# Hybrid DeltaNet and differential-attention block: where in a partition the moving operands of the 256-column products begin

## The chip, the cores and the metric

The kernel runs on one core of one Trainium2 chip. The metric is the device time of one execution, in microseconds. The kernel before takes 1933.78 us, the median of three runs (1933.39 to 1934.75 us).

A matrix product on TensorE has two operands in on-chip memory. One, here called the loaded operand, is put into the array ahead of the product (128 columns of it, an instruction of its own, shown as engine PEld). The other, the moving operand, streams through it (up to 512 columns). While one product streams, the operand of the next is being loaded.

## The reference, cut to what matters

One layer of a hybrid backbone over 1024 latent tokens with 256 context tokens ahead of them, model width 1024. One wide projection feeds two branches: a chunked gated DeltaNet with a short convolution (A) and a differential softmax attention with eight heads (B). Both are gated, projected, merged and mapped out.

```python
h = rms_norm(x) * (1.0 + scale[:, None]) + shift[:, None]
hc = rms_norm(ctx) * (1.0 + scale_c) + shift_c
qkv_a, z_a, a_raw, b_raw, q_b, k_b, v_b, z_b, gates = split_cols(h @ w_in)
...
o_a, o_ac = gdn_bidirectional(...)            # branch A
...
def block(qi):                                # branch B, 128 queries at a time
    s = jnp.einsum('bqhcd,bkhcd->bhcqk', qi, k).astype(jnp.float32) * scale
    p = jax.nn.softmax(s, axis=-1)
    attn = p[:, :, 0] - lam * p[:, :, 1]
    return jnp.einsum('bhqk,bkhv->bqhv', attn.astype(v.dtype), v)
...
merged = g_a * (y_a.reshape(b, length, GDN_WIDTH) @ w_oa) + g_b * (y_b.reshape(b, length, DIFF_V_WIDTH) @ w_ob)
return merged @ w_out
```

## The kernel before, in words

**Products in three passes.** The large products are made of float32r parts: each operand is split into a high part and a low remainder, and three products are summed, high by high, high by low and low by high. So for every block of 128 rows of the contraction there are three products.

**Two ways round.** For most of the projection the weights are loaded and the normed tokens `hs` move, 512 columns at a time (for the convolved q, k and v of branch A, and for the gates). For q, k and v of branch B it is the other way round: 128 tokens of `hs` are loaded and the weights `wh`, `wl` (high and low parts of 256 columns of the projection, tiles of 8 x 256 floats in a partition) move. These are the 256-column products of `part_flow`, and of the second column group of kind "t" in `conv_flow`. The first group of that kind carries 32 more columns for the gates of branch A, so its products have 288 columns.

**The stages, in the order of the profile.** The front (norms, modulation, the first weights), then the conv stage with 512-column products and the two groups of kind "t"; the parts stage to 734 us (four pairs of k, two of v, four of q, with the preparation of branch A between them), which the second group of kind "t" precedes from 398 us on; the scan stage to about 1290 us (the chunk recurrence `chain`, `out` in 128-column products, with the gate projections of 512 columns filling in); attention to about 1764 us (scores `s`, transposes `t`, values `v`, and the products `ma` of the projection of branch A filling in); then `mb` and the last projection `x`, `z`.

**Attention.** For each head and 128 queries, six pieces of scores: the queries' high part `qh` and then their low part `ql` is loaded, the keys `kk` move (512, 512 and 256 columns, for each of two softmaxes). VectorE scales the scores and takes their minimum (L1571), ScalarE exponentiates, VectorE, ScalarE and GpSimd combine the two softmaxes, TensorE transposes the result, ScalarE and VectorE split it in `ah` and `al` (L1640, L1645). For two blocks of 128 queries together, `att_out` makes 30 products of 256 columns: `vh` or `vl` loaded, `ah` or `al` moving.

**What sets the order.** The kernel orders its instructions itself while it is built. Every stream of work is a generator that names the engine, a cost and what it waits for, and a planner with modelled clocks takes the next one; the costs are numbers in the code (0.1195 for a product of 256 columns) and do not come from tile addresses. Semaphores are set by the framework from the tiles' places.

**Where tiles lie.** A pool gives each tag a place in every partition. The weights' tiles come from two pools, `wa` and `wb`; the queries, keys, values and softmax tiles from `a0`, `a1`, and for even heads the high queries and keys from the pool of branch A's preparation. In the program as built, the moving operand of each 256-column product of `part_flow`, of the second group of kind "t" and of `att_out` begins a whole multiple of 128 bytes away from the operand that is loaded while it streams. That also holds for the 512-column products of the projections. In the scores of even heads, the low queries `ql` begin 64 bytes off a multiple of 128 from the keys that stream while they are loaded; in those of odd heads they do not.

## Time and profile before

| what | value |
|---|---|
| median of three runs | 1933.78 us |
| the profiled execution's own time | 1933.29 us |
| its span, first to last instruction | 1931.2 us |
| granted TensorE clock | 1.000 |
| products on TensorE (records) | 13807 |
| 256-column products with weights moving (`mm<-wh,hs`, `mm<-wl,hs`) | 1632 + 816 |
| 256-column products with softmax tiles moving (`v<-ah`, `v<-al`) | 640 + 320 |
| the same weights moving with 288 columns | 160 + 80 |

How to read it: the records of products overlap, since the next product begins to stream before the last results of the one before have come out. A record's duration is therefore not what a product costs in a full stream; that is the distance from one start to the next. In the names, `out<-moving,loaded` for products and the same names for the loads (engine PEld). Waits of TensorE are those that end on another engine; two matters look alike in busy time, a wait inside the array and the streaming itself.

### The profile page before, as it was taken

The page shows a single profiled execution, that of the slowest core. Times are in us where ns is not written, and L with a number is a line of the kernel's source. Part 1 is how long each engine was busy: PE and PEld are TensorE (multiplying, and loading weights), DVE is VectorE, ACT ScalarE, POOL GpSimd, SP SyncE. Part 2 cuts the span into 40 slices and gives each one's busy share as a digit, 9 for nine tenths or more (in the row PEclk, how much of TensorE's full clock was granted, in tenths as well). Part 3 has the DMA queues.
Part 4 walks back from the last instruction along what each step waited for, and adds up shares of the span by engine and source line. Part 5 has one row for each costly group of instructions (what it writes and reads, how often), then busy time and mean ns, then how long its engine had stood idle before and what let it go on. Part 6 is the DMA issues. An engine that isn't in the chain of part 4 may idle for free.

```text
span 1931.2 us, 37500 instructions
## 1 busy us (share of the span) xinstructions
PE 1890.5 (98%) x13807; PEld 1665.9 (86%) x13807; DVE 1450.8 (75%) x3613; ACT 1075.3 (56%) x2237; POOL 678.1 (35%) x610
## 2 busy tenths in 40 slices
PE   6999999999999999999999999999999999999999
PEld 4888888899999998888888888888997888888887
DVE  4687998957887888867865865338996979995677
ACT  4543444426233564677576656448885868884222
POOL 3200000005441342343333332326766667672203
PEclk9999999999999999999999999999999999999999
DMA  9144535575545557667785575666336474226542
GB/s 335 60 135 98 138 95 136 124 193 175 166 142 182 183 191 229 227 195 234 210 290 176 196 200 154 219 226 225 131 123 208 158 240 150 92 88 213 191 153 87
DMA packets 383038, 336.39 MB, mean 174 GB/s; under 512 B 142609, under 2 KB 323443, under 8 KB 381831
## 3 DMA queue, kind: packets, MB, share of 16 engines
q1 hardware_dynamic: 382855, 333.99, 55.1%
q8 instruction: 109, 1.79, 0.4%
q14 instruction: 74, 0.61, 0.1%
HBM read 222.14 MB, written 111.79 MB: 173 GB/s over the span
## 4 chain that ended last, share of the span: by engine, by line
PE 82%; DVE 7%; DMA 4%; ACT 4%; issue 2%; POOL 1%; SPq 1%; ACTq 0%; DVEq 0%; POOLq 0%
PE mm L56 42%; PE s L56 7%; PE v L56 6%; PE chain L56 5%; PE mb L56 5%; PE ma L56 4%; PE x L56 3%; PE t L63 3%; PE out L56 3%; PE gram L56 1%; DVE S L1571 1%; DVE ac L595 1%; PE tr L63 1%; PE mp L56 1%; DMA hx<-tbd 1%
## 5 line engine op out<-in xcount | busy, mean ns | idle before, releaser
L56 PE MATMUL mm<-hs,wh 128*128 128x512 f32 (+1 forms) x2048 | 648.0, 389 | 1.5 <-DVE hs L408 1.4
L56 PEld LDWEIGHTS mm<-hs,wh 128*128 128x128 f32 x2048 | 371.0, 189 | 58.8 <-DVE hs L408 2.0
L56 PE MATMUL mm<-hs,wl 128*128 128x512 f32 (+1 forms) x1024 | 397.4, 388 | 1.0 <-POOL wl L886 1.0
L56 PE MATMUL mm<-wh,hs 128*128 128x256 f32 (+1 forms) x1792 | 332.7, 286 | 0.2 <-ACT sq L978 0.2
L56 PEld LDWEIGHTS mm<-wh,hs 128*128 128x128 f32 x1792 | 280.8, 191 | 0.7 <-ACT sq L978 0.4
L1571 DVE TENSOR_SCALAR_CACHE_REDUCE S<-s,rsq 128x512 f32<-128x512 f32 (+1 forms) x384 | 239.8, 655 | 28.0 <-PE s L56 25.1
L56 PE MATMUL mm<-wl,hs 128*128 128x256 f32 (+1 forms) x896 | 255.6, 285 | 0.0
L1608 POOL TENSOR_TENSOR S<-S 128x1280 f32<-128x1280 f32 x64 | 189.0, 2957 | 92.0 <-ACT S L1601 90.7
L56 PEld LDWEIGHTS mm<-hs,wl 128*128 128x128 f32 x1024 | 193.7, 189 | 29.8 <-POOL wl L886 1.4
L1584 ACT ACTIVATE S<-S,mn 128x1280 f32<-128x1280 f32 x128 | 175.2, 1372 | 51.8 <-DVE mn L1583 51.4
L56 PEld LDWEIGHTS mm<-wl,hs 128*128 128x128 f32 x896 | 171.3, 191 | 0.1
L595 DVE SCALAR_TENSOR_TENSOR ac<-xc,convT,ac 128x1284 f32<-128x1284 f32 (+1 forms) x96 | 138.8, 1449 | 12.9 <-ACT ac L593 12.2
L56 PE MATMUL s<-kk,qh 128*128 128x512 f32 (+1 forms) x384 | 142.6, 372 | 1.9 <-DVE S L1571 1.6
L56 PE MATMUL s<-kk,ql 128*128 128x512 f32 (+1 forms) x384 | 132.9, 358 | 0.5 <-DMA ql<-qd 0.5
L1645 DVE TENSOR_TENSOR al<-t,ah 128x512 fp32r<-128x512 f32 (+1 forms) x192 | 107.0, 596 | 7.3 <-ACT ah L1640 6.0
L580 POOL MEMSET xc<- 128x2 f32 (+1 forms) x64 | 3.6, 99 | 298.6 <-DMA gkk<-xc 120.4
L1160 DVE TENSOR_TENSOR ts<-ts,tmp 80x31 f32<-80x31 f32 (+15 forms) x248 | 94.6, 381 | 6.0
L1158 DVE TENSOR_TENSOR tmp<-ab,ts 80x31 f32<-80x31 f32 (+15 forms) x248 | 89.8, 362 | 6.6 <-DMA ab<-da 1.3
L56 PE MATMUL ma<-y,wh 128*128 128x512 f32 x256 | 93.0, 409 | 1.7 <-DVE g L1818 1.7
L1327 ACT ACTIVATE vd<-chain,edk 128x128 f32<-128x128 f32 x144 | 52.1, 369 | 75.8 <-PE chain L56 70.2
L1640 ACT CAST ah<-t 128x512 fp32r<-128x512 f32 (+1 forms) x192 | 87.9, 521 | 9.1 <-PE t L63 8.6
L56 PE MATMUL v<-al,vh 128*128 128x256 f32 x320 | 90.9, 284 | 0.7 <-DVE al L1645 0.6
(296 smaller groups left out, 4306.0 us busy)
## 6 DMA issues: line engine op xcount, KB each, us to landing
wr<-in_w_in_dram SPq DMA_DIRECT2D x48, 512.0 KB, 5.7
hx<-in_w_in_dram SPq DMA_DIRECT2D x64, 256.0 KB, 4.5
x<-xq SPq DMA_DIRECT2D x64, 256.0 KB, 4.8
X<-gcd SPq DMA_DIRECT2D x8, 1280.0 KB, 7.6
kd<-col SPq DMA_DIRECT2D x40, 256.0 KB, 2.2
xq<-X SPq DMA_DIRECT2D x16, 640.0 KB, 8.8
kk<-kd SPq DMA_DIRECT2D x16, 640.0 KB, 7.2
kq<-gkq SPq DMA_DIRECT2D x8, 1152.0 KB
```

Of the source, the lines that this page charges most:

```text
L56: self.nc.tensor.matmul(out, lhsT, rhs, start=start, stop=stop)
L63: self.nc.tensor.transpose(out, src, self.ident[:src.shape[0], :src.shape[0]])
L580: x["e"].append((yield PL1, 0.1, [old], lambda: nc.gpsimd.memset(xc[:, a:b], 0.0)))
L595: t = yield DV2, 1.21e-3 * wd, [t], lambda: nc.vector.scalar_tensor_tensor(ac[:, :wd], xc[:, j:j + wd], self.convw(j, x["ct"]), ac[:, :wd] ...
L1158: t = yield DV2, n * w / 960.0 + 0.08, [t if j else self.later(t, 2.5), t1], lambda: V.tensor_tensor(tv, ab[:, j + 1:, j:j + 1].to_broadca ...
L1160: t = yield DV2, n * w / 960.0 + 0.08, [t, t1], lambda: V.tensor_tensor(ts[:, j + 1:, :w], ts[:, j + 1:, :w], tv, ALU.subtract)
L1327: td = yield ACT, 0.251, [t], lambda: nc.scalar.activation(vd, pc[:, 1], AF.Copy, scale=self.edk[:, c, g:g + 1])
L1571: e = yield DVE, 0.675 if m == 512 else 0.408, [e, self.sfree[c].get(n - 4 + c)], lambda: self.nc.vector.tensor_scalar(x["S"][c][:, o:o + ...
L1584: x["x"].append((yield ACT, 1.36, [e], lambda: nc.scalar.activation(S, S, AF.Exp, bias=x["mn"][:, c:c + 1], scale=-1.0, accum_out=w["l0"][ ...
L1608: e = yield POOL, 2.9, [e], lambda: self.nc.gpsimd.tensor_tensor(S0, S0, S1, ALU.add)
L1640: e = yield ACT, 0.48 if nb == 4 else 0.27, [t, y["old", k]], lambda: self.nc.scalar.copy(y["ah", k][:, :, q], pv)
L1645: t = yield DVE, 0.603 if k < 2 else 0.322, [e, y["old", k]], lambda: self.nc.vector.tensor_tensor(y["al", k][:, :, q], pv, y["ah", k][:, ...
```

## The change

The tiles get a few more floats, and the parts of them that are used begin further on. Weights that will move start 8 floats (32 bytes) into their tile; weights that will be loaded start where the distance to `hs` stays a multiple of 128 bytes. `ah` and `al` start 8 floats in. `ql` of even heads starts 48 floats (192 bytes) in. In the program as built, the distance between the moving operand and the one being loaded goes from a multiple of 128 bytes to 32 bytes past one for the 256-column products of `part_flow`, of the second group of kind "t" and of `att_out` (3408 of them), and for `kk` against `ql` in even heads from 64 bytes off to a multiple. It stays as it was for the 288-column products, for the 256-column products in which `hs` moves, and for all 512-column ones.

Every engine's instructions stand in the same order before and after, on all five engines, line numbers aside. The places of some other tiles move by multiples of 64 bytes. Three waits differ on the SP queue, which issues the loads: that of `vv` for the first head also waits for the last product of the parts stage, since the two now share memory; the load of `sz` waits for a somewhat later product, on which the load of `wq` right behind it waited before; and the load of `yl` waits for a product 11 counts of TensorE's semaphore later.

```diff
+    def wtile(self, pool, name, moving=False):
+
+        o = (0, 8, 32, 8)[2 * (name == "wl") + moving] if pool is self.wa else (0, 8, 0, 8)[2 * (name == "wl") + moving]
+        return pool.tile([P, KT * W + (32 if pool is self.wa else 48)], F32R, tag=name, name=name)[:, o:o + KT * W].rearrange("p (k n) -> p k n", k=KT)
...
-                hl, ends = [self.wab[1 - i].tile([P, KT, n], F32R, tag=t, name=t) for t in ("wh", "wl")], []
+                hl, ends = [self.wtile(self.wab[1], t) if i == 0 else self.wab[0].tile([P, KT, n], F32R, tag=t, name=t) for t in ("wh", "wl")], []
...
-        self.stream(self.conv_weights([c for _, c in cols], pools), 3)
+        self.stream(self.conv_weights([c for _, c in cols], pools, [k not in range(3) for k, _ in cols]), 3)
...
-    def conv_weights(self, cols, pools):
+    def conv_weights(self, cols, pools, moving):
...
-                yield from self.weight(raw, *(pools[(i + 1) % 2].tile([P, KT, W], F32R, tag=n, name=n) for n in ("wh", "wl")),
+                pool = pools[(i + 1) % 2]
+                yield from self.weight(raw, *(self.wtile(pool, n, moving[i]) for n in ("wh", "wl")),
                                        c0, W, [self.part_t.get(i - 2)], self.parts_, i, (DV2, DV2))
...
-                self.wab = [self.spool(lw, "wa"), self.spool(cx, "wb")][::-1]
+                self.wa, wb = self.spool(lw, "wa"), self.spool(cx, "wb")
+                self.wab = [wb, self.wa]
...
-                ring = [self.wab[0].tile([P, 2, KT, P], F32R, tag=n, name=n) for n in ("wh", "wl")]
+                ring = [self.wtile(self.wab[0], n).rearrange("p (a b) (c n) -> p a (b c) n", a=2, c=2) for n in ("wh", "wl")]
...
-                yield from self.weight(raw, *(self.wab[i % 2].tile([P, KT, W], F32R, tag=n, name=n) for n in ("wh", "wl")),
+                yield from self.weight(raw, *(self.wtile(self.wab[i % 2], n, True) for n in ("wh", "wl")),
                                        self.part_cols(*p), W, [self.part_t.get(i - 2)], self.parts_, i, (POOL, DV2))
...
-        w["ql"] = self.a0.tile([P, 2, L], F32R, tag=f"ql{h % 2}", name="ql")
+        o = 48 if h % 2 == 0 else 0
+        w["ql"] = self.a0.tile([P, 2 * L + 64], F32R, tag=f"ql{h % 2}", name="ql")[:, o:o + 2 * L].rearrange("p (c n) -> p c n", c=2)
...
-            for a in ("ah", "al"):
-                y[a, k] = self.a1.tile([P, nb, W], F32R, tag=f"{a}{k}", name=a)
+            for a, o in (("ah", 8), ("al", 8)):
+                y[a, k] = self.a1.tile([P, nb * W + 64], F32R, tag=f"{a}{k}", name=a)[:, o:o + nb * W].rearrange("p (j n) -> p j n", j=nb)
```

## The prediction

> **What bounds the kernel now.** I read the page's engine totals first, then the chain of waits, then the busy time by stage.
>
> ```profile
> PE 1890.5 (98%) x13807; PEld 1665.9 (86%) x13807; DVE 1450.8 (75%) x3613; ACT 1075.3 (56%) x2237; POOL 678.1 (35%) x610
> PE 82%; DVE 7%; DMA 4%; ACT 4%; issue 2%; POOL 1%; SPq 1%; ACTq 0%; DVEq 0%; POOLq 0%
> 397.50:734.50 337.00, 333.03 (x3267) 329.19 (x3266) 263.53 (x631) 150.71 (x346) 115.28 (x88) 1.00 0.57 178
> 1290.00:1764.00 474.00, 466.74 (x2973) 409.42 (x2972) 394.86 (x1312) 369.41 (x612) 299.78 (x149) 1.00 0.49 165
> ```
>
> In the last two rows the columns after the window's length are PE, PEld, VectorE, ScalarE and GpSimd busy us, then the granted clock and the DMA share. The first is the stretch that holds all 256-column products with weights moving (the parts stage and the group ahead of it), the second attention. TensorE is never short of work for long: it is busy 333 of 337 us and 467 of 474. Busy there does not mean streaming, so the question is how far apart its products start. The chain in order of time has unbroken stretches that tell:
>
> ```profile
> 565.92 28.66 PE mm L56 x239
> 1764.09 87.04 PE mb L56 x384
> 1400.32 1.04 PE L63 MATMUL t<-ct,S 128*128 128x128 f32 x8
> 1401.66 0.38 PE L63 MATMUL t<-ct,S 128*128 128x128 f32 x2
> ```
>
> 239 products of 256 columns in 28.66 us start every 119.9 ns; 384 of 512 columns in 87.04 us every 226.7 ns. The difference is 106.8 ns for 256 columns, 0.417 ns a column. So the 256 columns themselves are 106.8 ns, and in both sizes about 13 ns a product are left over. That leftover is all the change can touch. The last two rows, of the timeline, say that six transposes more take 0.66 us more, 110 ns each; I use them below as a bound.
>
> **The leftover isn't the same at all times**, and this carries my forecast:
>
> ```profile
> L56 PE MATMUL mm<-wh,hs x1632: 277/283/385, 397.8 to 734.1; 128*128 128x256 f32 x182
> L56 PE MATMUL v<-ah,vh x320: 274/283/383, 1328.4 to 1752.2; 128*128 128x256 f32 x160
> L56 PE MATMUL v<-ah,vl x320: 274/282/287, 1329.2 to 1752.4; 128*128 128x256 f32 x160
> L56 PE MATMUL mm<-hs,wh x970: 387/392/499, 734.2 to 1290.0; 128*128 128x512 f32 x194
> L56 PE MATMUL mb<-yh,wh x128: 389/389/389, 1763.9 to 1850.3; 128*128 128x512 f32 x128
> ```
>
> These rows of the view by source line give least, median and greatest duration in ns. In a full stream a duration is the spacing plus what a product needs to come out: 283 stands with 119.9 and 389 with 226.7, so 163 and 162 ns. Read that way, the quickest 256-column products of the parts stage stood 277 - 163 = 114 ns from the next, the quickest of the values 111 ns, at the same shapes and the same distance between operands as the median of 120. In the 512-column products it is the other way: 389 throughout `mb`, but a median of 392 in the scan stage, where other products keep breaking the stream. So the leftover runs from about 4 to 13 ns for 256 columns, and a settled stream of 256 columns rests near the upper end of that, a settled one of 512 near its lower end. What is left to differ from product to product, as I read it, is how the streaming operand and the load beside it meet in time. An offset between their addresses moves that meeting too. No row before shows a 32-byte offset, so its effect has to be bounded.
>
> **The change part by part.**
>
> *How many products.* From the view of groups, shapes kept apart:
>
> ```profile
> L56 PE MATMUL mm<-wh,hs 128*128 128x256 f32 x1632 | 300.5, 285 | 0.2 <-ACT sq L978 0.2
> L56 PE MATMUL mm<-wl,hs 128*128 128x256 f32 x816 | 232.0, 284 | 0.0
> L56 PE MATMUL v<-al,vh 128*128 128x256 f32 x320 | 90.9, 284 | 0.7 <-DVE al L1645 0.6
> L56 PE MATMUL mm<-wh,hs 128*128 128x288 f32 x160 | 32.3, 295 | 0.0
> ```
>
> 2448 products with weights moving and 3 x 320 = 960 with softmax tiles moving: 3408 in all. The 288-column ones keep their distance and count for nothing.
>
> *Price of one.* Best case, the spacing falls to that of the transposes, 110 ns: 10 ns saved. Nearly the same is the least spacing of the values, 111. Worst case, the offset puts the stream where the 512-column products of the scan stage are, 392 against 389: 3 ns lost. Between them I take 115.5 ns, halfway from the quickest row (111) to the settled 120: 4.5 ns saved. I lean to the gain since for this width the settled state is the slow one, so that most other meetings in the rows are quicker. Then the parts stage and the group ahead of it save 2448 x 4.5 = 11.0 us and the values 960 x 4.5 = 4.3 us.
>
> *What of that reaches the end.* TensorE's order doesn't change, so what it saves moves all later work forward, as long as nobody else is late next. In the first stretch VectorE is busy 264 of 337 us; with 11 us less it is at 81%. Its work there comes in bursts (rope, splitting, the substitution), and TensorE's transposes wait for it:
>
> ```profile
> PE tr L63 <- DVE fin L1000: 1.2, 1, 1.2
> PE ma L56 <- DVE g L1818: 1.7, 2, 0.9
> PE s L56 <- DVE S L1571: 1.6, 6, 0.5
> ```
>
> These are waits of a few us in all, and I let them grow by 2 us in the parts stage. In attention VectorE is busy 395 of 474 us and ScalarE 369; scores wait for VectorE to empty a bank. A third of the 4.3 us may be lost there, 1.4. The scan stage holds none of these products; it only begins earlier.
>
> *Low queries of even heads.* Eight tiles by six pieces by four heads are 192 products whose next load moves.
>
> ```profile
> L56 PE MATMUL s<-kk,ql x384: 274/391/485, 1296.1 to 1731.9; 128*128 128x512 f32 x128, 128*128 128x256 f32 x64
> ```
>
> If they went from the middle of this row to 389, it would be 192 x 2 ns = 0.4 us; if the other way, as much lost. I take 0.
>
> *Waits and moved tiles.* The load of `vv` gains a wait for the last product of the parts stage, which begins at 734.1 us by the row above. The first of these loads leaves at 745.0 us, so the wait is over by then:
>
> ```profile
> L1273 SPq DMA_DIRECT2D vv<-gv x8: 368/430/2132, 745.0 to 1218.2; - x8
> ```
>
> The other two changed waits are for products that a neighbouring load waited for anyway. Engines write the shifted tiles as before: no row prices an offset for them, and they have room (ScalarE 151 of 337 us in the first stretch). I take 0.
>
> *Sum.* 11.0 + 4.3 - 2 - 1.4 = 11.9 us. The profiled execution took 1933.29 us (span 1931.2, 2.1 around it), 0.5 under the median of the runs. 1933.29 - 11.9 = 1921.4; by the median 1921.9. I say **1921.5 us**.
>
> **The rivals.**
>
> *No change.* The leftover is a fixed cost of a product: it is 13 ns at 256 and at 512 columns, and the median of the 288-column group (295 against 283 for 32 columns more, 0.38 ns each) fits that. The quick products would then be the stream making up time after a break. Time: 1933.5 us. Against it stand the 512-column rows, in which products after breaks are slower, not quicker. The Trainium skill speaks for this rival: "TensorE: Matmul & The Clock Gate", Part 2, says that TensorE has two independent read ports and that loading the next operand does not steal read bandwidth from the running product; by it the distance between the two would not matter at all. The trace agrees in that loads overlap products everywhere, but not in a leftover that varies at one shape. The same page's section on the back-to-back issue gap gives N/2.4 + 2.5 ns, so 109 ns for 256 columns; an estimate from that page is 3408 x 11 = 37 us if the whole leftover above it went, which no row shows for a product of this kind.
>
> *Partial.* The offset only keeps the stream from settling, and the spacing is near 118 (2 ns saved): 6.8 us, of which some 5.5 arrive. Time: 1928 us.
>
> *The whole leftover.* 10 ns on 3408 products is 34 us; the first stretch would then shrink by 24 of 337 us, VectorE would be at 84% of it and become late next, and I let a quarter be lost. Time: 1933.3 - 25 = 1908 us.
>
> *Slower.* The settled state at a whole multiple is the one to be in, as it is for 512 columns, and 32 bytes off is like the broken streams of the scan stage: 392 against 389 in the median, 3 ns on 3408 products, 10 us, all of it on TensorE's path. Time: 1944 us. It decides the sign as soon as the spacing is over 120 ns. Against it: at this width the trace's broken streams are the quicker ones.
>
> **How the numbers follow.** Forecast 0.37 (1921.5), partial 0.20 (1928), whole leftover 0.11 (1908), no change 0.18 (1933.5), slower 0.14 (1944). A difference of 0.2%, 3.9 us, is about what a measurement of this kernel tells from none. Faster takes the forecast, the whole leftover and most of partial: 0.66. Within 0.2% are no change, less a small part that would stray beyond, and the rest of partial: 0.19. Slower: 0.15. The forecast's own range is 1915 to 1927. The range that should hold 8 times in 10 reaches from the quick rival to just over no change, and leaves out most of the slower one: 1905 to 1937.
>
> **What would show it.** The durations of `mm<-wh,hs` at 128x256 in the parts stage tell most directly: a median of 278 to 279 in place of 283 is my forecast, 272 to 274 the whole leftover, 281 partial, 283 no change, over 283 slower. `v<-ah,vh` should move with it, while `mb` stays at 389, the 288-column group at 295 and the 512-column ones of the conv stage as they were. The parts stage, from the first of these products to the last, should be 8 to 9 us shorter, with waits of `tr` on VectorE somewhat longer than 1.2 us. I am wrong if the medians stay, if the weights' products and the values' move in different directions, or if the products get quicker and the waits for VectorE take the gain back.

## The result, and the profile after

The changed kernel takes 1929.63 us, the median of 14 runs (1926.13 to 1933.84), beside 1934.07 us for the kernel before in the same comparison (14 runs, 1929.43 to 1936.20). The ratio is 0.9983, with a 95% interval of 0.9976 to 0.9991: 3.3 us less, 1.7 to 4.6 by the interval; the two medians stand 4.4 us apart, inside it. That is a gain, but within the 0.2% that the prediction called no difference, and less than half of the 12 us that it forecast. 1929.6 us lies in the range that should hold 8 times in 10 (1905 to 1937), but outside the forecast's own (1915 to 1927). The profiled execution took 1929.92 us (span 1927.8), 3.4 us less than the one before.

These rows after the change answer those that the prediction showed: the page's busy times, rows of the chain of waits (start, length, engine, tile, line, count), and the view by source line (least, median and greatest duration in ns), and one of the view by windows (columns as in the prediction).

```profile
PE 1885.5 (98%) x13807; PEld 1659.8 (86%) x13807; DVE 1446.3 (75%) x3613; ACT 1076.1 (56%) x2237; POOL 678.3 (35%) x610
564.13 28.11 PE mm L56 x239
1760.73 87.04 PE mb L56 x384
L56 PE MATMUL mm<-wh,hs x1632: 274/280/390, 397.8 to 730.7; 128*128 128x256 f32 x182
L56 PE MATMUL v<-ah,vh x320: 274/280/382, 1325.8 to 1748.7; 128*128 128x256 f32 x160
L56 PE MATMUL v<-ah,vl x320: 274/280/287, 1326.6 to 1748.9; 128*128 128x256 f32 x160
397.50:731.10 333.60, 328.60 (x3267) 323.88 (x3266) 261.44 (x631) 151.04 (x346) 115.29 (x88) 1.00 0.58 179
```

The same 239 weight products now take 28.11 us in place of 28.66, so 117.6 ns each in place of 119.9; the 384 products of `mb`, whose operands were left alone, still take 87.04 us. The medians fell from 283 to 280 ns. The last row is the stretch of the weights' products with its end moved: it holds the same records as the one before, in 333.6 us in place of 337.0.

From the products' starts in the two traces, stage by stage (settled: products with neighbours of their own kind on both sides, for the weights those of the ten parts; the sums are over products that directly follow one another; the stretch of `v` also counts the one-column products that write it):

| where | before | after |
|---|---|---|
| settled weight products, a start every | 119.8 ns | 116.8 ns in one weight pool, 118.0 in the other |
| settled value products | 119.4 ns | 116.9 ns |
| sum over 2397 steps from weight product to weight product | 291.9 us | 286.6 us (-5.3) |
| first to last weight product | 336.25 us | 332.82 us (-3.4) |
| sum over 823 steps from value product to value product | 100.4 us | 99.0 us (-1.4) |
| first to last product of `v` | 425.79 us | 424.88 us (-0.9) |
| last weight product to first value product (scan stage) | 594.33 us | 595.15 us (+0.8) |

So products got closer by 6.7 us in all, and 4.3 us of it arrive at the ends of the two stages. Two things are to be explained: why the price of a product fell by 2 to 3 ns and not by 4.5, and where the other third went. The two weight pools differ for a plain reason: in one, high and low part both stand 32 bytes off; in the other the low part's tile begins an odd multiple of 128 bytes after the high part's, so that two steps in three have the distance 32 and the third has 160.

### The profile page after: what moved, and what is told of

It is laid out like the page before. It is cut to its first block, busy times and chain, and to the rows that moved or that the text cites. A ratio compares the mean times of both kernels' runs of the same rounds, so it can differ in the third digit from the quotient of the medians.

```text
span 1927.8 us, 37500 instructions
## 1 busy us (share of the span) xinstructions
PE 1885.5 (98%) x13807; PEld 1659.8 (86%) x13807; DVE 1446.3 (75%) x3613; ACT 1076.1 (56%) x2237; POOL 678.3 (35%) x610
## 4 chain that ended last, share of the span: by engine, by line
PE 80%; DVE 7%; DMA 5%; ACT 4%; issue 2%; POOL 1%; SPq 1%; ACTq 0%; DVEq 0%; POOLq 0%
PE mm L56 40%; PE s L56 7%; PE v L56 5%; PE chain L56 5%; PE mb L56 5%; PE ma L56 4%; PE x L56 3%; PE t L63 3%; PE out L56 3%; PE gram L56 1%; DVE S L1579 1%; DMA sk<-gkq 1%; DVE ac L601 1%; PE tr L63 1%; PE mp L56 1%
## 5 line engine op out<-in xcount | busy, mean ns | idle before, releaser
L56 PE MATMUL mm<-wh,hs 128*128 128x256 f32 (+1 forms) x1792 | 327.3, 283 | 0.3 <-ACT sq L985 0.3
L56 PEld LDWEIGHTS mm<-wh,hs 128*128 128x128 f32 x1792 | 276.8, 188 | 0.8 <-ACT sq L985 0.5
L601 DVE SCALAR_TENSOR_TENSOR ac<-xc,convT,ac 128x1284 f32<-128x1284 f32 (+1 forms) x96 | 138.6, 1447 | 11.3 <-ACT ac L599 10.7
L586 POOL MEMSET xc<- 128x2 f32 (+1 forms) x64 | 3.6, 101 | 297.3 <-ACT sq L635 113.8
```

The source lines that it names most:

```text
L56: self.nc.tensor.matmul(out, lhsT, rhs, start=start, stop=stop)
L586: x["e"].append((yield PL1, 0.1, [old], lambda: nc.gpsimd.memset(xc[:, a:b], 0.0)))
L601: t = yield DV2, 1.21e-3 * wd, [t], lambda: nc.vector.scalar_tensor_tensor(ac[:, :wd], xc[:, j:j + wd], self.convw(j, x["ct"]), ac[:, :wd] ...
```

## The experiments

**The distance, swept.** Other distances in the places that the change touches, and in `mb`. In the first sweep `at` is 4, 16, 40, 48, 56 floats for the five parts in one weight pool; in the second it is 44, 52, 24, 50, 60, the softmax tiles begin 24, 28, 36, 44, 46, 50, 52, 60 floats in, and `mb` is left alone.

```diff
-        o = (0, 8, 32, 8)[2 * (name == "wl") + moving] if pool is self.wa else (0, 8, 0, 8)[2 * (name == "wl") + moving]
+        if moving and pool is self.wa:
+            o = (32, 0)[name == "wl"]
+        elif moving:
+            o = at
+        else:
+            o = 32 if pool is self.wa and name == "wl" else 0
...
-            for a, o in (("ah", 8), ("al", 8)):
+            o = (0, 2, 4, 8, 16, 32, 48, 56)[y["h"]]
+            for a in ("ah", "al"):
...
-            hi, lo = (self.ws.tile([P, KT, P], F32R, tag=n, name=n) for n in ("wh", "wl"))
+            d = (0, 2, 4, 8, 16, 24, 28, 32)[m]
+            hi, lo = (self.ws.tile([P, KT * P + x], F32R, tag=n, name=n)[:, y:y + KT * P].rearrange("p (k n) -> p k n", k=KT) for n, x, y in (("wh", 32, d), ("wl", 0, 0)))
```

> The changed kernel with other distances between moving and loaded operand. The softmax tiles of head 0 to 7 begin 0, 8, 16, 32, 64, 128, 192, 224 bytes further on than a multiple of 256 (the loaded values at 0); the parts' weights, high and low alike, stand 128 bytes off in one buffer and 16, 160, 64, 192, 224 in turn in the other; in the last product (mb) the loaded high halves are shifted by 0 to 128 bytes, a different shift for each of eight column blocks. Theory A (the distance sets the spacing, and 32 bytes is only one value of it): at 0 the 256-column stream starts a product every 120.0 ns, at 32 bytes every 116.7, at the other distances between 111 and 120, and not the same everywhere. Theory B (any distance but 0 breaks the locked state): 120.0 at 0 and about 116.7 at all others. Theory C (a particular 32-byte place only): 116.7 at 32 and 224 bytes and 120 at the rest. For mb: if 512-column streams have the same lock, its 226.7 ns falls by about 3 ns at shifts other than 0; if not, it stays 226.7 throughout.

> The changed kernel with further distances: the softmax tiles of head 0 to 7 begin 96, 112, 144, 176, 184, 200, 208, 240 bytes past a multiple of 256, the parts' weights 128 bytes in one buffer, and 176, 208, 96, 200, 240 in turn in the other. By what was measured so far (120.0 ns at 0 and 8 bytes, 116.8 at 32 and 64, 118.8 at 128, 117.4 at 160, 115.8 at 192, 118.3 at 224) a smooth curve gives 117 to 118 at 96, 118 to 119 at 112 and 144, 116 to 117 at 176 and 208, and above 119 at 240. If the products meet in steps (of 64 bytes, say), neighbours such as 184, 192, 200 differ by more than 1 ns, and some distance is below 115.

Measured, as the mean distance of settled starts (number of steps behind it):

| distance, bytes past a multiple of 256 | weights moving | softmax tiles moving |
|---|---|---|
| 0 (before) | 119.8 ns (1862) | 119.4 ns (484) |
| 8 | | 120.2 (53) |
| 16 | 118.1 (215) | 117.1 (70) |
| 32 (the change) | 116.8 (1006) | 116.9 (484) |
| 64 | 116.8 (222) | 117.0 (73) |
| 96 | 120.0 (222) | 120.1 (62) |
| 112 | | 116.7 (53) |
| 128 | 118.9 (850) | 118.7 (48) |
| 144 | | 118.6 (70) |
| 160 | 117.4 (222) | |
| 176 | 119.2 (215) | 119.0 (58) |
| 184 | | 119.9 (73) |
| 192 | 115.8 (163) | 115.8 (47) |
| 200 | 120.2 (163) | 120.9 (48) |
| 208 | 119.2 (222) | 118.9 (47) |
| 224 | 118.3 (177) | 118.2 (73) |
| 240 | 117.2 (177) | 117.4 (73) |

The same can be read in the chain of waits, where one row (start, length, count) holds the same 95 products of the last q part in each kernel. Before, at distance 0:

```profile
714.51 11.40 PE mm L56 x95
```

After the change, at 32 bytes:

```profile
711.42 11.09 PE mm L56 x95
```

In the first sweep, at 224 bytes:

```profile
713.97 11.24 PE mm L56 x95
```

In the second, at 240 bytes:

```profile
713.97 11.13 PE mm L56 x95
```

120.0, 116.7, 118.3 and 117.2 ns a product, within 0.2 ns of the table. What follows: the spacing goes with the distance, and weights and values agree on it within 1 ns wherever both were tried. Theory B (anything but 0 will do) falls with 8, 96 and 200 bytes, theory C with 64 and 192; theory A stands, though 200 bytes go up to 0.9 ns over its 120. The smooth curve of the second expectation falls too: 184, 192 and 200 bytes give 119.9, 115.8 and 120.9 ns. Its other theory, steps, had neighbours more than 1 ns apart, as they are, but also some distance below 115 ns, and none is; steps of 64 bytes it is not, since 0, 64, 128 and 192 give four values. The change's 32 bytes are a middling place; of those tried, 192 is the best.

The distance doesn't settle it to the last nanosecond. At 0 every part has a mean of 119.7 to 120.0 ns. At 32 bytes for both halves four parts have 116.7, one 117.4, and the group of kind "t" 117.8.

In `mb`, rows of the sweep by source line and in the chain of waits:

```profile
L56 PE MATMUL mb<-yh,wh x128: 389/394/399, 1762.3 to 1850.4; 128*128 128x512 f32 x128
L56 PE MATMUL mb<-yl,wh x128: 387/390/401, 1762.5 to 1850.6; 128*128 128x512 f32 x128
1762.48 88.76 PE mb L56 x384
```

Any shift made the 512-column products slower: 88.76 us for 384 in place of 87.04. In the column blocks with a shift the mean step was 229.0 to 233.4 ns, though one step in three was still at distance 0; before it was 226.7 throughout. In the five blocks that are shifted throughout, the steps with the next load shifted and the product's own not took 232.5 ns, those the other way round 229.3: it is mainly the load beside the product that counts. So the two widths want different things, and that the change left the 512-column operands alone was needed.

**The place or the distance.** Two kernels. The first shifted hidden states and values:

```diff
-        self.hs[g] = [pool.tile([P, KT, n], F32R, tag=f"s{g}{i}", name="hs") for i in range(2)]
+        self.hs[g] = [pool.tile([P, KT * n + 8 * (g < 1)], F32R, tag=f"s{g}{i}", name="hs")[:, 8 * (g < 1):8 * (g < 1) + KT * n].rearrange("p (k n) -> p k n", k=KT) for i in range(2)]
...
-                    v = w[n, k] = self.a0.tile([P, (r.stop - r.start) // P, P], F32R, tag=f"{n}{k}", name=n)
+                    o = 8
+                    v = w[n, k] = self.a0.tile([P, r.stop - r.start + 8], F32R, tag=f"{n}{k}", name=n)[:, o:o + r.stop - r.start].rearrange("p (t c) -> p t c", c=P)
...
-            for a, o in (("ah", 8), ("al", 8)):
+            for a, o in (("ah", 8 * (y["h"] < 4)), ("al", 8 * (y["h"] < 4))):
```

> Both operands shifted. The loaded values begin 32 bytes on in all heads; the softmax tiles begin 32 bytes on in heads 0 to 3 (distance 0) and at 0 in heads 4 to 7 (distance -32). The hidden states of the first four token tiles begin 32 bytes on too, so that the parts' products of these tiles are back at distance 0 in one weight buffer, and the 512-column products of the conv stage that stream them stand 32 bytes from their weights. If the distance counts: heads 0 to 3 at 120.0 ns, heads 4 to 7 at 116.7; parts' products of the first four token tiles 120.0, of the others 116.7. If the place of the moving operand itself counts: heads 0 to 3 at 116.7, heads 4 to 7 at 120.0, parts' products 116.7 everywhere. The 512-column products of the conv stage stay at 226.7 ns if this width has no such lock, and fall by some 3 ns if it has.

For the values and the parts this told nothing: tiles take up their size rounded to 32 bytes, so with 8 floats more in each the tiles behind them moved as well, and the distances became a mixture that differs from tile to tile (values 117.1 to 118.8 ns, parts 116.7 to 118.3). For the conv stage it did tell: there two of three steps had distance -32 in the first four token tiles and the rest stayed at 0.

```profile
276.41 46.83 PE mm L56 x226
L56 PE MATMUL mm<-hs,wh x1020: 277/392/795, 24.4 to 400.0; 128*128 128x512 f32 x126, 128*128 128x256 f32 x44
```

In the kernel before, the same 226 products stood at distance 0:

```profile
274.50 46.27 PE mm L56 x226
L56 PE MATMUL mm<-hs,wh x1020: 277/389/795, 24.3 to 396.9; 128*128 128x512 f32 x126, 128*128 128x256 f32 x44
```

46.83 us in place of 46.27, and the shifted 512-column products some 233 ns apart in place of 227: slower again, where the expectation had no change or a gain.

The second kernel moved all value tiles together, by one small tile laid behind them, and put each head's softmax tiles at a chosen distance:

```diff
+                    if (h, k, i) == (0, 2, 1):
+                        self.a0.tile([P, 8], F32, tag="gap", name="gap")
...
-            for a, o in (("ah", 8), ("al", 8)):
+            o = 56 if y["h"] < 4 else 0 if y["h"] < 6 else 40
+            for a in ("ah", "al"):
```

> The changed kernel with the loaded values (vh, vl) moved too: they now begin 224 bytes past a multiple of 256. The softmax tiles begin at 224 in heads 0 to 3 (distance 0), at 0 in heads 4 and 5 (distance 32), at 160 in heads 6 and 7 (distance 192). If the distance counts: 119.4 ns, 116.8 ns and 115.8 ns a product. If the place of the moving operand alone counts: by the sweep 118.2 ns at 224, 119.4 at 0, 117.4 at 160.

Rows by source line for the heads 0 to 3, 4 and 5, 6 and 7 in turn:

```profile
L56 PE MATMUL v<-ah,vh x160: 274/282/382, 1326.7 to 1539.7; 128*128 128x256 f32 x160
L56 PE MATMUL v<-ah,vh x80: 274/280/366, 1548.2 to 1654.1; 128*128 128x256 f32 x80
L56 PE MATMUL v<-ah,vh x80: 276/280/364, 1661.5 to 1749.6; 128*128 128x256 f32 x80
```

Settled starts came every 119.5, 117.0 and 115.6 ns, against 119.4, 116.8 and 115.8 by the distance and 118.2, 119.4 and 117.4 by the place. It is the distance between the moving operand and the loaded one, not where either lies. (Medians tell 120 from 117 but no longer 117 from 115.6, since at 192 bytes the products alternate between shorter and longer steps; starts are the better measure.)

**Is VectorE's load what takes the rest?** The prediction let TensorE's waits on VectorE grow. In the parts VectorE is busy 78% on the average. In a pair of kernels its largest piece of work there, the triangular substitution, was cut down; the same edit in the kernel before and in the changed one:

```diff
-                tv, ab[:, j + 1:, j:j + 1].to_broadcast([80, n, w]), ts[:, j, :w].unsqueeze(1).to_broadcast([80, n, w]), ALU.mult)
+                tv[:, :1, :1], ab[:, j + 1:j + 2, j:j + 1], ts[:, j:j + 1, :1], ALU.mult)
...
-            t = yield DV2, n * w / 960.0 + 0.08, [t, t1], lambda: V.tensor_tensor(ts[:, j + 1:, :w], ts[:, j + 1:, :w], tv,
+            t = yield DV2, n * w / 960.0 + 0.08, [t, t1], lambda: V.tensor_tensor(ts[:, j + 1:j + 2, :1], ts[:, j + 1:j + 2, :1], tv[:, :1, :1],
...
-        t1 = yield PL1, 0.06, [t1], lambda: nc.gpsimd.memset(ts.rearrange("p a b -> p (a b)")[:, 0:1024:33], 1.0)
+        t1 = yield PL1, 0.06, [t1], lambda: nc.gpsimd.memset(ts.rearrange("p a b -> p (a b)")[:, 0:1024:33], 0.0)
```

> The kernel before, with the triangular substitution left out: its 62 VectorE operations a head keep their places and waits but work on one column, and its result is set to zero, so that the delta-rule branch gives zero and the output is another one. VectorE loses about 9 us of work for each of the four heads whose substitution falls into the parts stage. It is the partner of the next kernel. From the first 256-column weight product to the last should take 334 us instead of 336.3, since TensorE's waits there on VectorE are a few us in all.

> The changed kernel with the same substitution left out. If VectorE being late next is what took part of the parts stage's saving (products 5.2 us closer together, stretch only 3.3 us shorter), then with VectorE relieved the stretch from the first to the last 256-column weight product should be 4.7 to 5.5 us shorter than in the partner, and its waits for transposes should not differ by more than 0.5 us. If something else takes it (DMA, the order of TensorE's work), the difference stays near 3.3 us.

The stretch took 334.04 us in the partner, as expected, and 331.26 us in the changed one: 2.8 us less, not 4.7 to 5.5. (Each of these is one profile; two kernels whose weight products stand alike differ by 0.3 to 0.4 us in this stretch, as the table of the two halves below shows.) VectorE had 30 us less to do (231 and 235 us busy in place of 263), and still the waits grew. TensorE's waits for transposes in the parts, by the view of waits (us, times, longest), in the partner:

```profile
PE tr L63 <- DVE Z L1221: 0.4, 1, 0.4
PE tr L63 <- POOL fin L1008: 0.2, 1, 0.2
```

And in the changed kernel without the substitution:

```profile
PE tr L63 <- DVE fin L1007: 1.2, 2, 0.9
PE tr L63 <- DVE Z L1228: 0.4, 1, 0.4
PE tr L63 <- POOL fin L1015: 0.3, 1, 0.3
```

By the starts, the steps from a weight product to a transpose grew by 2.2 us. Theory fallen: how busy VectorE is does not decide.

**Or the fixed way from a bank to its transposes?** A transpose of k waits for a chain: last product of a bank, ScalarE's copies and squares, VectorE's sums and rope, GpSimd's scaling with the norm. Its first and last operation and the transposes behind them, in the timeline of the changed kernel:

```profile
485.98 0.65 ACT L984 COPY raw<-mm 128x256 f32<-128x256 f32 x2 [4.25 <-issue]
491.15 1.05 POOL L1015 TENSOR_TENSOR fin<-fin,ss 128x512 f32<-128x512 f32 x1 [1.30 <-DVE fin L1007]
492.25 0.66 PE L63 MATMUL tr<-ct,fin 128*128 128x128 f32 x4
```

6.2 us from ScalarE's start to GpSimd's end, and TensorE does 48 products of the next bank meanwhile, 5.6 us, and a few more. Each operation of this chain takes as long as before. So where the transposes were ready just in time, 48 products that are 2 to 3 ns shorter make TensorE arrive 0.1 us early. The pair cuts the last step of the chain down:

```diff
             te = [(yield POOL, 1.05, [te, tw], lambda: Q.tensor_tensor(
-                f8, f8, ss.rearrange("p t g -> p (t g)").unsqueeze(2).to_broadcast([P, 8, 64]), ALU.mult))]
+                f8[:, :, :1], f8[:, :, :1], ss.rearrange("p t g -> p (t g)").unsqueeze(2), ALU.mult))]
```

> The kernel before, with GpSimd's last step ahead of the transposes of k (fin times its norm) done on one column of 64 only, so that the normalisation of k is left out and the output is another one. The way from a bank's last product to its transposes gets about 0.9 us shorter. Partner of the next kernel; TensorE's waits for transposes in the parts stage should nearly vanish, and the stretch from the first to the last 256-column weight product takes about 334.5 us in place of 336.3.

> The changed kernel with the same step left out. Theory: what takes part of the saving in the parts stage is the fixed time from a bank's last product through ScalarE, VectorE and GpSimd to its transposes (some 6.4 us) against 48 products that TensorE does meanwhile (5.6 us); with the products 2 to 3 ns closer each such wait grows by 0.1 us, however busy VectorE is. With the way 0.9 us shorter the waits for k's transposes stay away in both kernels, and the stretch is 4.3 to 5.2 us shorter than in the partner (3.4 with the step, 2.8 with the substitution left out). Rival: the loss lies elsewhere, and the difference stays at 2.8 to 3.5 us.

As a whole it missed: 335.47 us in the partner, 331.93 us in the changed one, 3.5 us less. By place it held. The starts, part by part:

| difference, changed minus its partner | with the whole chain | chain shortened |
|---|---|---|
| k and first v parts, with the group of kind "t": steps between weight products | -3.0 us | -2.7 us |
| the same: steps to and between transposes | +0.8 us | 0.0 us |
| the same stretch as a whole | -2.2 us | -2.6 us |
| last v and first q part: steps to transposes | +0.7 us | +0.7 us |
| other q parts: steps to transposes | +0.4 us | +0.5 us |

Where the shortened chain runs (k), the growth is gone, and all that the products save arrives. Where it does not run (q is scaled elsewhere), the loss is what it was. The expectation had put the whole loss on k. The 0.4 to 0.5 us at the other q parts were not taken apart. What stands at the first q part is seen in the waits of VectorE and TensorE there, before the change:

```profile
DVE sq L998 <- DMA hx<-tbd: 3.1, 1, 3.1
PE tr L63 <- DVE fin L1000: 1.2, 1, 1.2
```

And after it, with the transfer's row from the chain of waits:

```profile
DVE sq L1005 <- DMA hx<-tbd: 3.7, 1, 3.7
PE tr L63 <- DVE fin L1007: 1.9, 1, 1.9
621.17 11.30 DMA hx<-tbd
```

q's rotary tables can only be fetched when the last v part has read the context tokens for the last time, and take 11.3 us to land (11.05 before); that time doesn't shrink either. The wait that the prediction quoted as one on VectorE (`fin`, 1.2 us) has this transfer behind it, but not alone. In the timeline before, one of VectorE's operations on these tables takes 2.62 us where its like take 0.42, and it ends 0.3 us after an operation of GpSimd that began ahead of it:

```profile
634.92 0.43 DVE L998 TENSOR_TENSOR sq<-raw,hx 128x256 f32<-128x256 f32 x1 [3.11 <-DMA hx<-tbd]
636.11 2.63 POOL L886 TENSOR_TENSOR wl<-wr,wh 128x1024 fp32r<-128x1024 f32 x1 [2.51 <-ACT wh L885]
636.40 2.62 DVE L999 TENSOR_TENSOR fin<-raw,hx 128x256 f32<-128x256 f32 x1
639.53 0.66 PE L63 MATMUL tr<-ct,fin 128*128 128x128 f32 x4 [1.20 <-DVE fin L1000]
```

After the change the same happens to the operation at L1007:

```profile
633.05 2.45 POOL L893 TENSOR_TENSOR wl<-wr,wh 128x1024 fp32r<-128x1024 f32 x1 [2.52 <-ACT wh L892]
633.29 2.50 DVE L1007 TENSOR_TENSOR fin<-fin,sq 128x256 f32<-128x256 f32 x1
```

So 2.1 to 2.2 us of the way to these transposes, more than TensorE waits for them, are not the transfer's. No run took that operation of GpSimd away.

**The two halves alone.** Weights moved and softmax tiles not (first piece of the difference), and the other way round (second); the low queries of even heads back in both (third).

```diff
-            for a, o in (("ah", 8), ("al", 8)):
+            for a, o in (("ah", 0), ("al", 0)):
...
-        o = (0, 8, 32, 8)[2 * (name == "wl") + moving] if pool is self.wa else (0, 8, 0, 8)[2 * (name == "wl") + moving]
+        o = (0, 0, 32, 32)[2 * (name == "wl") + moving] if pool is self.wa else (0, 0, 0, 0)[2 * (name == "wl") + moving]
...
-        o = 48 if h % 2 == 0 else 0
+        o = 0
```

> The changed kernel with the softmax tiles and the low queries back at a multiple of 256 bytes; only the parts' weights stay moved. If the two halves of the change act apart: the stretch of the weights' products is 332.8 us (before 336.3, changed 332.8), attention from the first value product to the last 425.8 (before 425.8, changed 424.9), and the scan stage between them 0.5 to 0.9 us longer than before, since its work that waits for transfers begins earlier and the transfers don't. If that longer scan stage is scatter from run to run, it is as likely as short as before (594.3).

> The changed kernel with the parts' weights and the low queries back at a multiple of 256 bytes; only the softmax tiles stay moved. If the halves act apart: stretch of the weights' products 336.3 us, attention 424.9 us, scan stage 594.3 us as before; the whole about 0.9 us under the kernel before in its profiled execution.

| | before | changed | weights only | values only |
|---|---|---|---|---|
| weight products, first to last | 336.25 us | 332.82 | 333.25 | 336.55 |
| scan stage | 594.33 us | 595.15 | 593.78 | 593.06 |
| products of `v`, first to last | 425.79 us | 424.88 | 425.73 | 424.91 |

The halves act apart, 3.0 to 3.4 us and 0.9 us. The scan stage, where the changed trace had 0.8 us more, is shorter than before in both halves; over all kernels in which nothing there was touched it lies between 592.9 and 595.3 us. So that 0.8 us is scatter.

**A better distance.** All moving operands of 256 columns 192 bytes on, in both weight pools; the low part's tile in the second pool now begins where its distance is the same:

```diff
-        o = (0, 8, 32, 8)[2 * (name == "wl") + moving] if pool is self.wa else (0, 8, 0, 8)[2 * (name == "wl") + moving]
-        return pool.tile([P, KT * W + (32 if pool is self.wa else 48)], F32R, tag=name, name=name)[:, o:o + KT * W].rearrange("p (k n) -> p k n", k=KT)
+        o = (0, 48, 16, 0)[2 * (name == "wl") + moving] if pool is self.wa else 48 * moving
+        return pool.tile([P, KT * W + ((16 if name == "wl" else 48) if pool is self.wa else 48)], F32R, tag=name, name=name)[:, o:o + KT * W].rearrange("p (k n) -> p k n", k=KT)
...
-            for a, o in (("ah", 8), ("al", 8)):
+            for a, o in (("ah", 48), ("al", 48)):
```

> The changed kernel with every moving operand of 256 columns 192 bytes on (weights of the parts in both buffers, high and low alike, and the softmax tiles), the distance with the closest products in the sweep. By the sweep a settled stream starts a product every 115.8 ns in place of 116.8 (one weight buffer, values) and 118.0 (the other buffer). 1006 x 1.0 + 856 x 2.2 ns, and a quarter more for the products that were not counted as settled, is 3.6 us on the weights, about 0.8 us on the values. If about half is lost to work that is late next, as in the change itself, some 2.2 us arrive: a ratio to the kernel before of 0.9971. If all of it arrives: 0.9960. If nothing more arrives because other work now sets the pace: 0.9983, as the change.

1926.39 us, 0.9974 of the kernel before (0.9964 to 0.9984), 3 parts in 10,000 from the value expected with half lost. The interval also reaches the change's 0.9983, so these times alone do not show a gain over the change; the profile does (span 1924.0 us in place of 1927.8). Weight products settle at 115.4 ns over the ten parts, value products at 115.9, and the 95 products of the last q part run at 113.6 ns (a row of the chain of waits, then two of TensorE's waits in the parts):

```profile
710.45 10.79 PE mm L56 x95
PE tr L63 <- DVE fin L1007: 2.5, 3, 1.5
PE tr L63 <- POOL fin L1015: 0.9, 3, 0.5
```

The steps between weight products are now 10.4 us shorter than before, and the stretch 4.9 us. Of the 5.5 us between them 4.4 are in steps to and between transposes: the waits have grown further, on VectorE's `fin` (1.2 us before) and on GpSimd's (0.2 us before). The other 1.1 us lie among the small products of branch A's preparation in the last v part, where TensorE's wait before `p` was 0.6 us and is now 2.0; why is open.

**The tables fetched earlier.** The same, and in the last v part the context tokens come first, so that the transfer can leave while the part runs:

```diff
-            if parts[i - 1][0] != kind == "q":
-                self.hx = self.hc.tile([P, 2, L], F32, tag="s20", name="hx")
-                self.rope["q"] = self.hx[:, 0].rearrange("p (a b t f) -> p a b t f", a=2, b=2, f=32), (
-                    yield DMA, 1.5, [self.part_t[i - 1]], lambda: self.nc.sync.dma_start(self.hx[:, 0], self.tbd[0]))
-            for t0 in range(0, NL if kind == "q" else NT, 2):
+            for t0 in range(0, NL, 2) if kind == "q" else (8, 0, 2, 4, 6) if parts[i + 1][0] == "q" else range(0, NT, 2):
...
+                if t0 == 8 and parts[i + 1][0] == "q":
+                    self.hx = self.hc.tile([P, 2, L], F32, tag="s20", name="hx")
+                    self.rope["q"] = self.hx[:, 0].rearrange("p (a b t f) -> p a b t f", a=2, b=2, f=32), (
+                        yield DMA, 1.5, [t], lambda: self.nc.sync.dma_start(self.hx[:, 0], self.tbd[0]))
```

> The version with all moving operands 192 bytes on, and in the last value part the two context tiles come first in place of last, so that the transfer of q's rotary tables, which waits for these tiles' hidden states to be read for the last time, is issued some 20 us earlier. In the runs so far it landed 11.3 us after its issue at the end of the part, VectorE waited 3.7 us for it and the transposes behind it 1.1 to 2.1 us. Theory: the fixed delay at this place takes part of what faster products save; without it the first q part gets 1.5 to 2 us shorter, and the ratio to the kernel before goes from 0.9974 to about 0.9965. Rival: the earlier transfer delays others, or another fixed chain is late at once, and the ratio stays at 0.997 to 0.998.

1924.44 us beside 1933.38, 0.9953 (0.9940 to 0.9966). It beats both kernels: the one before by 9 us, and the changed one, by their two ratios, by some 6. The stretch of the weights' products fell from 331.4 to 328.0 us. The transfer is now issued at 590.0 us, and VectorE's wait for it is gone from the profile. Its row by tile, and TensorE's waits for transposes in the parts:

```profile
L960 SPq DMA_DIRECT2D hx<-tbd x1: 341/341/341, 590.0 to 590.0; - x1
PE tr L63 <- DVE fin L1007: 1.8, 3, 1.0
PE tr L63 <- POOL fin L1015: 0.9, 3, 0.5
```

The ratio came out below the 0.9965 expected, which lies just inside the interval, but not by the expected way. The first q part alone got 0.4 us shorter, not 1.5 to 2. Last v part and first q part together took 1.8 us less than with 192 bytes alone; by the starts 0.8 us of that are in steps to and between transposes, and 1.2 us are weight products that stood closer, 113.6 and 114.7 ns apart in place of 116.8 in both, at the same distance. The next two q parts took 1.3 us less as well. The planner had ordered the work around them anew, and how much of all this is due to the tables was not separated.

## Why the prediction was wrong, step by step

*TensorE sets the pace, and the leftover is what can be touched.* Right. TensorE is still busy for 98% of the span, the products' smaller steps do arrive where no fixed chain stands, and the 512-column stage `mb` stayed at 87.04 us to the hundredth.

*The leftover depends on how the two operands' addresses meet.* Right, against the rival "no change". Here the measurement also decides on the Trainium skill. "TensorE: Matmul & The Clock Gate", Part 2, has the loading of the next operand on a read port of its own, so that it takes no read bandwidth from the running product. In these runs the distance between the two operands alone moved the settled start from 115.4 to 120.9 ns at 256 columns and from 226.7 to 233.4 ns at 512. Loads do overlap products, but in these streams their place is not indifferent to them.

*The price of one product, 115.5 ns.* This is the step that failed. It was taken halfway between the settled 120 and the quickest single products (111), as if any other meeting of the two were likely to be as good as a break in the stream. At 32 bytes the stream settles anew, at 116.8 ns, and with every third step at 160, as in 1104 of the 2448 weight products, at 118.0. Over all steps from weight product to weight product the gain was 2.2 ns, over those of values 1.7 ns, not 4.5: 5.3 + 1.4 us where 11.0 + 4.3 were put down. The rival "partial" had priced this at 2 ns and 6.8 us; 6.7 were measured, and its time of 1928 us is the nearest to the 1929.6 measured, though by its account the stream would not settle at all. With 2.4 us lost on the way, 4.3 us are left where 11.9 were forecast. The value taken was no wild one (at 192 bytes the settled step is 115.4 ns, and the weights' steps 10.4 us shorter), but nothing in the trace before tied it to 32 bytes. The least durations also were those of rare products: of the 2397 steps before, 2085 took 120 ns, 221 took 116 to 119, and only 8 took 113 or 114. Taken from the starts, the price of leaving 120 would have been 2 to 3 ns. Nor did the prediction weigh that in one weight pool the two parts would stand at different distances, which the program as built shows.

*Two us lost to waits of transposes in the parts.* Right in size (1.9 us) by luck, wrong in its ground. It argued from VectorE's share of busy time, and the substitution's removal showed that the growth of these waits does not hang on it. What matters for k is a fixed time (a chain over three engines) against a number of products that has become shorter; that the transfer for q acts alike is read from its rows and was not isolated. Thus the loss grows with the gain: 1.9 us of 5.3 here, at 192 bytes 5.5 of 10.4, of which 4.4 at transposes. The prediction's loss of 2 us on 11 would have been too small by far had its price been right.

*1.4 us lost in attention.* 0.5 of 1.4 was lost: a third, as assumed, of a gain that was a third of the one put down. The ground given, scores that wait for VectorE, is not seen: TensorE's two waits there that the prediction quoted stayed within 0.1 us, so the share is luck, and what took the 0.5 us is open.

```profile
PE ma L56 <- DVE g L1826: 1.8, 2, 1.0
PE s L56 <- DVE S L1579: 1.7, 6, 0.5
```

*Low queries of even heads at nothing.* Right: 232.6 ns from high to low queries before, 232.5 after (512 columns, even heads).

*Signs.* Medians of 280 lay between those of the forecast (278 to 279) and of "partial" (281); weights and values moved together; `mb` and the 288-column group stayed; the waits of `tr` got longer. The stretch was to be 8 to 9 us shorter and was 3.4.

*The other rivals.* "Slower" had the right idea for the wrong width: off a whole multiple the 512-column products are slower by 2 to 7 ns, the 256-column ones by 1 ns at most (200 bytes) and mostly quicker. "The whole leftover" was not reached at any distance tried; the best mean, 115.4 ns, keeps 8.6 of 13.

## What to carry to other kernels

A stall of a fixed size per product is worth measuring against the operands' places: read the distance of starts in settled runs, vary the distance in one kernel (a different one per head or part costs a single profile), and only then choose, since neighbours 8 bytes apart differed by 4 to 5 ns here and one width wants what the other doesn't. When the pacing engine gets faster, don't look at the others' shares of busy time but at fixed ways back to it, engine to engine or by a transfer, whose slack was a number of its instructions: each such place can hand back part of what they save. And where two tiles are meant to stand alike, look up in the built program whether they do.

## What the runs showed that was not expected

- The settled step of 256-column products takes values from 115.4 to 120.9 ns with the distance of moving and loaded operand, without a plain order: 184, 192 and 200 bytes give 119.9, 115.8 and 120.9. Why is open; no run here looks inside a product.
- For 512-column products the distance 0 is the best of those tried (226.7 ns), and 32 to 240 bytes cost 2 to 7 ns, though not all steps were shifted alike in these runs. In the scores of even heads, where unlike products follow one another, going from 192 bytes to 0 changed nothing.
- At one distance a settled stream can run in more than one way. Its steps repeat in short patterns: at 32 bytes 116, 117, 117 ns in the last q part, 113, 116, 117, 120 in an earlier one, with the same mean. At 192 bytes 1295 of 2244 settled steps took 113 or 114 ns and 825 took 117 or 118, and the means of the parts run from 113.8 to 117.0 (113.3 in the group of kind "t"); a run of 95 products took 113.6 ns each. What chooses between the ways is open.
- A VectorE operation was drawn out by 2.1 to 2.2 us where it met one of GpSimd's (2.50 and 2.62 us in place of 0.42). It lies on the way to the transposes of the first q part, before the change and after.
